# Two layers of a hybrid decoder on one core: norm weights folded into tables, score maps joined, mixer order and both ends rewritten

## The chip, the cores and the metric

The kernel runs on one core of a Trainium2 chip. The metric is the device time of one launch in microseconds (us), as the median of several runs. Where a profile is shown, it is one execution taken by the hardware profiler; its span runs from the first to the last instruction of the program. PE is TensorE, ACT is ScalarE, DVE is VectorE, SP is the queue that issues most transfers.

## What is computed

Two layers, a sequence of 256 positions, a model width of 1024. In each layer the normed input `xn` goes through one joined projection `W_in`, whose columns feed four token mixers; their outputs are gated, summed and projected, and a gated feed-forward block and a gated per-layer embedding follow:

```python
def reference(...):
    for i in range(DEPTH):
        xn = rms_norm(h, norm_mix[i])
        u = xn @ w_in[i]
        (a_x, a_g, b_u, c_q, c_k, c_v, d_q, d_k, d_v, i_q, i_k, i_w) = jnp.split(u, IN_SPLITS, axis=-1)
        o_a = rg_lru_branch(a_x, a_g, ...)            # conv4, gated linear recurrence, GeLU gate
        o_b = conformer_branch(b_u, ...)              # GLU, causal conv31, RMSNorm, swish
        o_c = diff_attention_branch(c_q, c_k, c_v, ...)   # q, k normed with weights, partial rotary
        o_d = sparse_attention_branch(d_q, d_k, d_v, i_q, i_k, i_w, ...)   # indexer, top 64 keys
        mixed = sum(sigmoid(xn @ w_gate[i, j]) * (o_j @ w_branch[i, j]) for j in 0..3)
        h = h + mixed @ w_out[i]
        f = causal_dwconv(rms_norm(h, norm_ffn[i]) @ w_up[i], ...)
        h = h + (silu(f_gate) * f_val) @ w_down[i]
        e = rms_norm(p[i] @ w_ple_in[i], ple_norm[i])
        h = h + sigmoid(rms_norm(h, ple_gate_norm[i]) @ w_ple_gate[i]) * e
    return h
```

## The kernel before

**Products.** Every large product is made of three: both operands are split into a high half `hi` and a rest `lo` of a reduced 32-bit type, and hi·hi, hi·lo and lo·hi are summed. `mm3` (L263, products L271 to L273) holds the weights and streams 256 positions; it serves the units that want channels on the partitions (conformer value and gate `bv`/`bg`, recurrence inputs `a`, the feed-forward `up`). `tok_unit` (L302, products L314 to L316) holds 128 positions and streams 512 weight columns, for both halves `b` of the sequence in turn.

**Weights.** They come as 339 pieces of 128x1024 floats (512 KB). `prep_one` (L203) loads one on SP's queue (L215), makes `hi` by a copy on ACT (L216) and `lo` by a subtraction on DVE (L217). There are five buffers for raw pieces, six for split ones, and `take` keeps three pieces ahead.

**Order.** `unit_list` (L67) sets the order of the units: `bv`/`bg` pairs, the first half of the embedding, `dq`, `dk`, `ik`, `cq`, `ck`, `cv`, eight `a` units, then gates and branches by `MIX_ORDER` (L33), `out`, the second half of the embedding, 22 pairs of `up`, `down`, `pg`. The small work of the mixers (recurrence `side_a` L863, conformer `side_b` L920 with the conv taps L916, differential attention `side_c` L729, sparse attention `side_d` L577) is written as generators. After each piece `pump` (L234) adds 2.6 to each generator's account and lets it take a step for every `EVERY` of its own (L37); before a branch unit `drain` (L247) runs what is left of its mixer. A scheduler then settles the order on each engine from the order of the code and its waits.

**Start.** ACT's queue loads all per-channel vectors of layer 0 (L166, 128x365). On SP's queue come x in four loads of 256 KB (L465), the first piece in two halves, two more pieces, the constants (L469), the four tiles of h (L472), the embedding's gain and its input. Nineteen products of a tile of ones (L188) run ahead. x is multiplied by the norm's weight on ACT (L372, `hi`) and DVE (L373, `lo`); the norm's sums come from squares of h (L360).

**End.** The last unit (`pg`, n=1) sums both halves b over all eight k in turn; then ACT's tanh (L1104), two DVE steps (L1105, L1106) and the output transfers on ACT's queue (L1109) follow, each in two steps of 256 columns:

```python
for c in range(0, 512, step):
    A.activation(t[:, cs], bank[:, cs], AF.Tanh, scale=hr2[:, b:b + 1])
    V.scalar_tensor_tensor(t[:, cs], t[:, cs], 1.0, e[b][n][:, cs], op0=ALU.add, op1=ALU.mult)
    V.scalar_tensor_tensor(h[b][n][:, cs], t[:, cs], re[:, b:b + 1], h[b][n][:, cs], op0=ALU.mult, op1=ALU.add)
    if last:
        nc.scalar.dma_start(out_dram[:, b, n * 512 + c:n * 512 + c + step], h[b][n][:, cs])
```

Of the kernel before, what the change touches and what calls it, by code (L numbers as in the profile page):

```python
# [10 lines left out]
F32 = mybir.dt.float32  # L11
# [21 lines left out]
MIX_ORDER = (("gate", MIX[0]), ("gate", MIX[1]), ("branch", MIX[0]), ("gate", MIX[2]), ("branch", MIX[1]),  # L33
             ("gate", MIX[3]), ("branch", MIX[2]), ("branch", MIX[3]))


EVERY = {0: 4.8, 1: 5.1, 2: 3.3, 3: 2.9, 4: 5.5}  # L37
# [4 lines left out]
for _n, _w in (("norm_mix", 8), ("norm_ffn", 8), ("ple_gate_norm", 8), ("conv_a_w", 16),  # L42
               ("conv_a_b", 4), ("lru_b_r", 4), ("lru_b_i", 4), ("lru_lambda", 4), ("conv_b_w", 124),
               ("conv_b_b", 4), ("conv_b_norm", 4), ("conv_f_w", 132), ("conv_f_b", 44), ("diff_subln", 1)):
    _V[_n] = (_o, _w)
    _o += _w
# [5 lines left out]
for _n, _w in (("diff_q_norm", 64), ("diff_k_norm", 64), ("diff_lq1", 64), ("diff_lk1", 64), ("diff_lq2", 64),  # L52
               ("diff_lk2", 64), ("spa_q_norm", 128), ("spa_k_norm", 128), ("idx_k_norm", 32)):
    _R[_n] = (_o, _w)
    _o += _w
# [11 lines left out]
def unit_list(l):  # L67
# [19 lines left out]
    for n in range(4):  # L87
        bu(n)
    if not l:
        u.append(ple_in[0])  # L90
# [6 lines left out]
    for n in range(8):  # L97
        chan(("a", n), "w_in", n * P)
# [7 lines left out]
    for n in range(2):  # L106
        tok(("out", n), n * 512, n * 512 + 512, "w_out")
    u.append(ple_in[1])
# [15 lines left out]
def decoder_kernel(ctx: ExitStack, tc: tile.TileContext, w_dram, x_dram, xt_dram, p_dram, vec_dram, row_dram,  # L124
# [10 lines left out]
    RAW_BUFS, SPLIT_BUFS, LEAD, NBIG = 5, 6, 3, 37  # L135
# [3 lines left out]
    def nm(s):  # L139
        cnt[0] += 1  # L140
        return f"{s}_{cnt[0]}"

# [11 lines left out]

    def score_banks(Kw):
# [10 lines left out]
    nc.scalar.dma_start(vec[0], vec_dram[0])  # L166
    ones = cst.tile([P, P], F32, name="ones", tag="ones")
    V.memset(ones, 1.0)
    eps = cst.tile([P, 2], F32, name="eps", tag="eps")
# [15 lines left out]

    warm = smbank()
    for _ in range(19):
        T.matmul(warm[:, 0, :], ones, ones, start=True, stop=True)  # L188
# [14 lines left out]
    def prep_one():  # L203
        if nxt[0] >= len(stream):
            return
# [6 lines left out]
        step = m // 2 if i == 0 else m  # L212
        for c in range(0, m, step):
            cs = slice(c, c + step)
            nc.sync.dma_start(raw[:, cs], w_dram[i, :, cs])  # L215
            A.activation(hi[:, cs], raw[:, cs], AF.Copy)  # L216
            last_lo[0] = V.tensor_tensor(lo[:, cs], raw[:, cs], hi[:, cs].bitcast(F32), op=ALU.subtract).ins  # L217
        ready.append((hi[:, :m].rearrange("p (k n) -> p k n", k=nk), lo[:, :m].rearrange("p (k n) -> p k n", k=nk)))

# [121 lines left out]
    def rnorm(acc, scale, bias):  # L341
# [6 lines left out]
        return spread(rt)  # L348

    class Norm:  # L350
# [43 lines left out]

        def half(self):
# [22 lines left out]
    def rope(t, H, W, tab, b):  # L418

        rot = W // 4  # L420
        half = rot // 2
        q = t[:, :, 0:rot]
        cs = tab[:, b, 0, :][:, None, :].to_broadcast([P, H, rot])
        sn = tab[:, b, 1, :]
        t1 = st([P, P], "rp1", 2)[:, :H * rot].rearrange("p (h r) -> p h r", h=H)
        t2 = st([P, P], "rp2", 2)[:, :H * rot].rearrange("p (h r) -> p h r", h=H)
        V.tensor_tensor(t1, q, cs, op=ALU.mult)
        V.tensor_tensor(t2[:, :, 0:half], q[:, :, half:rot], sn[:, None, 0:half].to_broadcast([P, H, half]), op=ALU.mult)
        V.tensor_tensor(t2[:, :, half:rot], q[:, :, 0:half], sn[:, None, half:rot].to_broadcast([P, H, half]), op=ALU.mult)
# [9 lines left out]
    def gain_row(l):  # L439
        t = cst.tile([P, D], F32, name=nm("gain"), tag="gain")  # L440
        nc.sync.dma_start(t, gain_dram[l:l + 1, :].to_broadcast([P, D]))
        return t


    for l in range(L):
        vv = vec[l]
        rr = cst.tile([P, NR], F32, name=nm("row"), tag="row")
        lam_init = 0.8 - 0.6 * math.exp(-0.3 * l)

        def vcol(name):  # L450
            o, w = _V[name]
            return vv[:, o:o + w]
# [5 lines left out]

        if l == 0:
            nxt_nrm = Norm(vcol("norm_mix"))  # L460
            for i in range(4):
                if i == 2:
                    prep_one()
                x_ = bt()
                nc.sync.dma_start(x_, x_dram[:, 2 * i:2 * i + 2, :])  # L465
                nxt_nrm.split(i, x_)
            for _ in range(LEAD - 1):
                prep_one()
            nc.sync.dma_start(con, const_dram)  # L469
            for b in range(2):  # L470
                for n in range(2):
                    nc.sync.dma_start(h[b][n], xt_dram[:, b, n * 512:n * 512 + 512])  # L472
            ph = load_p(0)
        if l == 0:
            gr = gain_row(0)
        pk = [(ph[0][:, k, :], ph[1][:, k, :]) for k in range(2)]
        e = [[None, None], [None, None]]
        se = st([P, 2, 2], "se", 2)

        def embed(n):  # L480
            for b, bank in enumerate(tok_unit(pk, 1)):
                junk = bt().rearrange("p a b -> p (a b)")
                A.activation(junk, bank, AF.Square, accum_out=se[:, n, b:b + 1])
                e[b][n] = bt().rearrange("p a b -> p (a b)")
# [710 lines left out]
```

## Time and profile before

| what | us |
|---|---|
| median of 3 runs | 1048.24 (1047.9 to 1049.01) |
| the profiled execution's own time | 1050.01 |
| its span | 1048.2 |
| PE, DVE, ACT busy in it | 1032.0, 843.3, 690.3 |

The mean granted clock of TensorE in this execution is 0.992 of its full speed. Busy times of PE are modelled from the starts of pipelined products, so a busy PE may still wait inside a product's span; where that matters the starts of two neighbouring products are compared.

### The profile page before, as it was taken

To read this page: it belongs to the slowest core of one execution; us is meant where nothing else is said; L and a number is where in the kernel's file an instruction comes from. 1 tells how busy PE (TensorE), PEld (TensorE's weight loads), DVE (VectorE), ACT (ScalarE), POOL (GpSimd) and SP (SyncE) were. 2 spreads that over 40 slices of the span, in tenths; PEclk is the share of its full clock that TensorE was granted. 3 is DMA by queue.
4 is the path that set the end of the run, shared out by engine and by line. 5 is a ranking of instruction groups with operands and counts; after the bars stand their busy time and mean duration, and the time that the engine had idled before them with its cause. 6 is when DMAs were issued, how large, how long until landed. Compare 5 with 4: busy or idle time off the path is not lost.

```text
span 1048.2 us, 16586 instructions
## 1 busy us (share of the span) xinstructions
PE 1032.0 (98%) x6118; PEld 907.0 (87%) x6118; DVE 843.3 (80%) x1574; ACT 690.3 (66%) x1200; POOL 0.2 (0%) x4
## 2 busy tenths in 40 slices
PE   8999999999999999999999999999999999999997
PEld 7988977788889999988898888777888899999886
DVE  6888999988878978755676889999778799877453
ACT  6765778868557766644675668787784676665443
POOL 0000000000000000000000000000000000000000
PEclk8999999999999999999999999999999999999999
DMA  9765345654765665666656653445556556656641
GB/s 340 270 198 175 113 134 151 191 162 142 219 176 188 182 184 177 187 208 188 187 168 203 188 169 103 137 146 179 161 190 189 164 184 178 187 186 188 189 156 41
DMA packets 52784, 185.42 MB, mean 177 GB/s; under 512 B 5856, under 2 KB 6624, under 8 KB 52704
## 3 DMA queue, kind: packets, MB, share of 16 engines
q1 hardware_dynamic: 51696, 183.14, 56.9%
q10 hardware_dynamic: 1008, 1.24, 0.4%
q8 instruction: 48, 0.79, 0.3%
q14 instruction: 32, 0.26, 0.1%
HBM read 183.30 MB, written 1.05 MB: 176 GB/s over the span
## 4 chain that ended last, share of the span: by engine, by line
PE 82%; DVE 11%; ACT 4%; DMA 1%; issue 1%; SPq 0%; DVEq 0%; ACTq 0%
PE mm L314 17%; PE mm L316 17%; PE mm L315 16%; PE mm L272 9%; PE mm L271 9%; PE mm L273 9%; DVE lo L217 3%; DVE b L916 2%; ACT hi L216 1%; DMA raw<-in_w_dram 1%; DVE s L645 1%; DVE b L854 1%; DVE s L652 1%; PE sp L777 1%; DVE s L651 1%
## 5 line engine op out<-in xcount | busy, mean ns | idle before, releaser
L217 DVE TENSOR_TENSOR lo<-raw,hi 128x1024 fp32r<-128x1024 f32 (+1 forms) x339 | 411.7, 1216 | 142.4 <-ACT hi L216 140.0
L216 ACT ACTIVATE hi<-raw 128x1024 fp32r<-128x1024 f32 (+1 forms) x339 | 355.5, 1055 | 253.0 <-PE mm L316 154.9
L314 PE MATMUL mm<-hi,b 128*128 128x512 f32 x864 | 344.8, 399 | 0.1
L315 PE MATMUL mm<-lo,b 128*128 128x512 f32 x864 | 338.2, 391 | 2.6 <-DVE lo L217 2.6
L316 PE MATMUL mm<-hi,b 128*128 128x512 f32 x864 | 337.6, 391 | 0.0
L271 PE MATMUL mm<-b,hi 128*128 128x256 f32 x976 | 277.6, 286 | 2.3 <-ACT hi L216 1.8
L273 PE MATMUL mm<-b,lo 128*128 128x256 f32 x976 | 276.5, 284 | 1.0 <-DVE lo L217 1.0
L272 PE MATMUL mm<-b,hi 128*128 128x256 f32 x976 | 276.1, 284 | 0.1
L315 PEld LDWEIGHTS mm<-lo,b 128*128 128x128 f32 x864 | 163.0, 189 | 35.8 <-DVE lo L217 3.5
L316 PEld LDWEIGHTS mm<-hi,b 128*128 128x128 f32 x864 | 162.8, 188 | 34.3
L271 PEld LDWEIGHTS mm<-b,hi 128*128 128x128 f32 x976 | 187.5, 193 | 5.4 <-ACT hi L216 2.3
L314 PEld LDWEIGHTS mm<-hi,b 128*128 128x128 f32 x864 | 162.9, 189 | 33.5 <-ACT b L257 1.0
L273 PEld LDWEIGHTS mm<-b,lo 128*128 128x128 f32 x976 | 188.1, 193 | 1.4 <-DVE lo L217 1.4
L272 PEld LDWEIGHTS mm<-b,hi 128*128 128x128 f32 x976 | 187.9, 193 | 0.6 <-DVE b L373 0.4
L916 DVE SCALAR_TENSOR_TENSOR b<-s,vec,b 128x256 f32<-128x256 f32 x240 | 105.0, 477 | 0.0
L1069 DVE SCALAR_TENSOR_TENSOR s<-mm,vec,s 128x255 f32<-128x255 f32 (+1 forms) x144 | 59.5, 474 | 3.0 <-ACT s L1063 3.0
L257 ACT ACTIVATE b<-b 128x512 fp32r<-128x512 f32 x40 | 25.1, 628 | 22.9 <-DVE b L1073 18.5
L258 DVE TENSOR_TENSOR b<-b,b 128x512 fp32r<-128x512 f32 x40 | 27.5, 687 | 11.8 <-ACT b L257 11.8
L1063 ACT ACTIVATE s<-mm,vec 128x256 f32<-128x256 f32 x72 | 36.1, 552 | 0.0
L1072 ACT ACTIVATE s<-s 128x256 f32<-128x256 f32 x44 | 17.8, 409 | 8.7 <-DVE s L1069 8.6
L785 ACT ACTIVATE s<-sp,s,s 128x128 f32<-128x128 f32 (+1 forms) x32 | 16.0, 514 | 8.3 <-DVE s L782 8.3
L989 ACT ACTIVATE b<-mm,s 128x512 f32<-128x512 f32 x32 | 20.9, 690 | 0.8 <-PE mm L316 0.6
(216 smaller groups left out, 763.3 us busy)
## 6 DMA issues: line engine op xcount, KB each, us to landing
raw<-in_w_dram SPq DMA_DIRECT2D x337, 512.0 KB, 4.1
b<-in_x_dram SPq DMA_DIRECT2D x4, 256.0 KB, 6.4
h<-in_xt_dram SPq DMA_DIRECT2D x4, 256.0 KB, 6.2
gain<-in_gain_dram SPq DMA_DIRECT2D x2, 512.0 KB, 5.2
b<-in_lru_dram SPq DMA_DIRECT2D x4, 256.0 KB, 5.1
row<-in_row_dram SPq DMA_DIRECT2D x2, 336.0 KB, 4.5
raw<-in_w_dram SPq DMA_DIRECT2D x2, 256.0 KB, 5.0
b<-in_p_dram SPq DMA_DIRECT2D x2, 256.0 KB, 5.8
```

What stands on the lines that cost most here:

```text
L216: A.activation(hi[:, cs], raw[:, cs], AF.Copy)
L217: last_lo[0] = V.tensor_tensor(lo[:, cs], raw[:, cs], hi[:, cs].bitcast(F32), op=ALU.subtract).ins
L258: V.tensor_tensor(lo, src, hi.bitcast(F32), op=ALU.subtract)
L271: T.matmul(out, a, xh, start=first and k == 0, stop=False)
L272: T.matmul(out, a, xl, start=False, stop=False)
L273: T.matmul(out, b, xh, start=False, stop=last and k == nk - 1)
L314: T.matmul(outs[b], xk[k][0][:, bs], wh[:, kk, :], start=k == 0, stop=False)
L315: T.matmul(outs[b], xk[k][0][:, bs], wl[:, kk, :], start=False, stop=False)
L316: T.matmul(outs[b], xk[k][1][:, bs], wh[:, kk, :], start=False, stop=last)
L916: V.scalar_tensor_tensor(t, ypad[:, c, d:d + S], w[:, 31 * c + d:31 * c + d + 1], t, op0=ALU.mult, op1=ALU.add)
L1063: A.activation(cf[:, 2 * q + s_, :], bank[:, s_, :], AF.Identity, scale=w[:, 3 * c + 2:3 * c + 3], bias=bb[:, c:c + 1])
L1069: V.scalar_tensor_tensor(t, bank[:, s_, :S - d], w[:, 3 * c + 2 - d:3 * c + 3 - d], t, op0=ALU.mult, op1=ALU.add)
```

## The change

1. **Start.** x comes as eight loads of 128 KB, each followed by half a piece of 256 KB; the first four pieces hold two rows of k for four channel groups each (`bvg`), so that four `bv`/`bg` units run together, k by k. Only the norm's weight (128x8) is loaded ahead on ACT's queue; vectors, most constants, h, embedding input and gain come later. Ten products of ones instead of nineteen. The first norm's sums are taken from x in channel layout (`channel_finish`: squares, sums and a product with ones). The first half of the embedding of layer 0 moves behind the `out` units.
2. **Norm weights.** The q and k weights of both attentions are folded into the rotation tables and, for the columns that are not rotated, into the scale of the copy after the transpose. The multiplications L668 and L751 go; `rope` makes one product on a swapped view instead of two. The softmax scale goes into the per-head scale.
3. **Score maps.** For the first half of the sequence the indexer's two groups and the four heads of the differential attention each share banks and instructions.
4. **Order.** The `a` units move ahead of `dq`; `side_a` starts there. Gates 0, 3 and 2 come ahead of the first branch. `EVERY[2]` is 3.4 and `EVERY[3]` 3.2 (3.3 and 2.9 before). Layer 1's small values are made at the end of layer 0. Big buffers: 43 instead of 37.
5. **End.** The last unit makes half b=0 whole, then b=1 in two parts of 256 columns, each over all k (`tok_parts`); the outputs are issued by SP.

```diff
-MIX_ORDER = (gate 0, gate 3, branch 0, gate 2, branch 3, gate 1, branch 2, branch 1)
+MIX_ORDER = (gate 0, gate 3, gate 2, branch 0, gate 1, branch 3, branch 2, branch 1)
@@ unit_list
+        u.append((("bvg", 0), "w_in", [(k, 2, [(c, c + P) for c in (1024, 1536, 1152, 1664)]) for k in range(0, KD, 2)]))
+    for n in range(8):
+        chan(("a", n), "w_in", n * P)
     tok(("tok", "dq"), 3584, 4096)
...
-    for n in range(8):
-        chan(("a", n), "w_in", n * P)
@@ start
-    for _ in range(19):
+    for _ in range(10):
         T.matmul(warm[:, 0, :], ones, ones, start=True, stop=True)
...
+            nxt_nrm = Norm(gain0)
+            for k in range(KD):
+                if k % 2 == 0:
+                    x0.append(bt())
+                dma(x0[-1][:, k % 2, :], x_dram[:, k, :])
+                nxt_nrm.split(k // 2, x0[-1], (k % 2,))
+                prep_part()
...
+                for q in range(4):
+                    mm3(bbanks[q // 2][:, q % 2, :], wk, xs, q * P, k == 0 and q % 2 == 0, k + 1 == KD and q % 2 == 1)
...
+                if (l, c, j) == (0, 2, 0):
+                    nrm.channel_finish(x0)
@@ rope
-        V.tensor_tensor(t2[:, :, 0:half], q[:, :, half:rot], ...)
-        V.tensor_tensor(t2[:, :, half:rot], q[:, :, 0:half], ...)
+        V.tensor_tensor(t2.rearrange(two, u=2), q.rearrange(two, u=2)[:, :, ::-1, :], sn.rearrange(two, u=2), op=ALU.mult)
@@ side_d heads, side_c heads
-                for hh in range(4):
-                    q = dq[b][:, hh * P:(hh + 1) * P]
-                    V.scalar_tensor_tensor(q, q, ms[:, b, hh:hh + 1], rcol("spa_q_norm"), op0=ALU.mult, op1=ALU.mult)
...
-                V.tensor_tensor(v3, v3, rcol(gain)[:, None, :].to_broadcast([P, 8, 64]), op=ALU.mult)
...
+                    A.activation(dst[m][:, :, b * P:(b + 1) * P], tp[:, 2 * m:2 * m + 2, :], AF.Copy,
+                                 scale=vcol(f"diff_{gain}_col"))
@@ side_c
-            for b in range(2):
-                yield from weave(attend(b, hp) for hp in range(2))
+            yield from weave([*two_heads(1), attend(0, (0, 1))])
+            yield from weave(attend(1, (hp,)) for hp in range(2))
@@ end
+    def tok_parts(xk, npieces):
+        pcs = take(npieces)
+        for b, c, n in ((0, 0, 512), (1, 0, 256), (1, 256, 256)):
...
+            yield b, c, bank
...
-                        nc.scalar.dma_start(out_dram[:, b, n * 512 + c:n * 512 + c + step], h[b][n][:, cs])
+                        for dst, src in outs:
+                            nc.sync.dma_start(dst, src)
```

How the instructions stand at three places, before and after. First SP's queue at the start of the program: `raw` is a piece of weights, `b` from `in_x_dram` is x, `con` the constants, `h` the residual. Before:

```order
L465 DMA b_106<-in_x_dram 128x512
L215 DMA raw_122<-in_w_dram 128x512 x2
L215 DMA raw_147<-in_w_dram 128x1024
L215 DMA raw_153<-in_w_dram 128x1024
L465 DMA b_114<-in_x_dram 128x512
L469 DMA con<-in_const_dram 128x610
L472 DMA h_70<-in_xt_dram 128x512
L472 DMA h_71<-in_xt_dram 128x512
L472 DMA h_72<-in_xt_dram 128x512
L465 DMA b_131<-in_x_dram 128x512
```

After, from the last pair of x and weights on (seven such pairs, 128x256 and 128x512, stand ahead of it):

```order
L150 DMA b_152<-in_x_dram 128x256
L150 DMA raw_158<-in_w_dram 128x512
L150 DMA con<-in_const_dram 128x128
L150 DMA raw_200<-in_w_dram 128x1024
L150 DMA vec_75<-in_vec_dram 128x368
L150 DMA raw_231<-in_w_dram 128x1024
L150 DMA raw_261<-in_w_dram 128x1024
L150 DMA raw_292<-in_w_dram 128x1024
L150 DMA con<-in_const_dram 128x482
```

The wide loads of constants, vectors and h between the pieces have moved behind the last of x; h stands further down than these rows.

Second DVE in layer 0, in the stretch where the two attentions and the recurrence run beside the token units, at the rotation of one key or query tile. Before (L651 and L652 are the top-k search, L883 and L885 the recurrence, L217 the next piece's `lo`):

```order
L651 MAX s_1622<-s_1212 128x8
L751 TENSOR_TENSOR b_857<-b_857,row_104 128x512
L652 MATCH_REPLACE s_1213<-s_1622,s_1212 128x256
L427 TENSOR_TENSOR s_1629<-b_857,con 128x128
L651 MAX s_1625<-s_1213 128x8
L428 TENSOR_TENSOR s_1630<-b_857,con 128x8x8
L652 MATCH_REPLACE s_1212<-s_1625,s_1213 128x256
L429 TENSOR_TENSOR s_1630<-b_857,con 128x8x8
L883 SCALAR_TENSOR_TENSOR b_1550<-b_1550,b_1172 128x512
L430 TENSOR_TENSOR b_857<-s_1629,s_1630 128x8x16
L885 SCALAR_TENSOR_TENSOR b_1552<-b_1551,b_1552 128x512
L217 TENSOR_TENSOR lo_1649<-raw_1647,hi_1648 128x1024
```

After, at the same kind of tile (L491 to L493 are the rotation, L1002 the conformer's taps, L747 the top-k search, L538 a small value, L233 `lo`):

```order
L1002 SCALAR_TENSOR_TENSOR b_509<-s_172,vec_75,b_509 128x256 x2
L1002 SCALAR_TENSOR_TENSOR b_510<-s_172,vec_75,b_510 128x256 x2
L747 MATCH_REPLACE s_1480<-s_1656,s_1481 128x128
L491 TENSOR_TENSOR s_1671<-b_1297,s_503 128x128
L492 TENSOR_TENSOR s_1672<-b_1297,s_503 128x128
L233 TENSOR_TENSOR lo_1684<-raw_1682,hi_1683 128x1024
L493 TENSOR_TENSOR b_1297<-s_1671,s_1672 128x8x16
L491 TENSOR_TENSOR s_1727<-b_1184,s_501 128x128
L492 TENSOR_TENSOR s_1728<-b_1184,s_501 128x128
L538 TENSOR_TENSOR s_4938<-s_4938 128x4
L493 TENSOR_TENSOR b_1184<-s_1727,s_1728 128x8x16
L233 TENSOR_TENSOR lo_1709<-raw_1707,hi_1708 128x1024
```

The weight product ahead of the rotation is gone, the rotation is three rows instead of four, and the recurrence's rows are not there any more: they stand among earlier units. Two `lo` stand among these twelve rows, where one stood.

Third ACT in layer 0 at the conformer's norm, which needs the squares of two tiles (L928 before, L1014 after) and whose sums PE then makes. Before (L836 copies attention outputs, L989 is a gate's tanh):

```order
L836 ACTIVATE b_2613<-sp_2645,s_442 128x2x128
L836 ACTIVATE b_2615<-sp_2645,s_442 128x2x128
L216 ACTIVATE hi_2749<-raw_2748 128x1024
L836 ACTIVATE b_2613<-sp_2680,s_442 128x2x128
L836 ACTIVATE b_2615<-sp_2680,s_442 128x2x128
L216 ACTIVATE hi_2773<-raw_2772 128x1024
L928 ACTIVATE b_2731<-b_534 128x512
L928 ACTIVATE b_2732<-b_535 128x512
L216 ACTIVATE hi_2799<-raw_2798 128x1024
L989 ACT_TABLE_LOAD
```

After (L914 is a root, L921 the scaling of the differential attention's heads, L291 a split):

```order
L914 ACT_TABLE_LOAD
L914 ACTIVATE s_1858<-s_1858,eps 128x8
L1014 ACTIVATE b_2647<-b_509 128x512
L921 ACTIVATE b_1856<-b_1856,s_1858 128x128 x4
L291 ACTIVATE b_2266<-sp_2604 128x2x128
L921 ACTIVATE b_1857<-b_1857,s_1858 128x128 x3
L291 ACTIVATE b_2268<-sp_2604 128x2x128
L921 ACTIVATE b_1857<-b_1857,s_1858 128x128
L1014 ACTIVATE b_2648<-b_510 128x512
L232 ACTIVATE hi_2698<-raw_2697 128x1024
L232 ACTIVATE hi_2733<-raw_2732 128x1024
L389 ACTIVATE s_2656<-sp_2653,eps 128x2
```

The two squares stood next to each other; now the second stands behind eight scalings and two splits.

## Rows read from the trace of the kernel before

**Rows 1.** The page, part 1: engine, busy us (share of the span) xinstructions.
```profile
PE 1032.0 (98%) x6118; PEld 907.0 (87%) x6118; DVE 843.3 (80%) x1574; ACT 690.3 (66%) x1200; POOL 0.2 (0%) x4
```

**Rows 2.** Windows by stage: stretch, us, busy of each engine, PEclk, DMA share, GB/s.
```profile
0.00:20.00 20.00, 15.97 (x90) 14.71 (x91) 12.51 (x46) 10.88 (x20) 0.20 (x4) 0.83 0.92 339
100.00:140.00 40.00, 40.00 (x279) 36.16 (x278) 39.70 (x101) 31.10 (x59) 0.00 (x0) 1.00 0.38 118
140.00:230.00 90.00, 87.20 (x429) 69.45 (x428) 85.19 (x202) 68.11 (x151) 0.00 (x0) 0.98 0.54 162
656.00:746.00 90.00, 87.30 (x429) 69.59 (x428) 84.25 (x195) 67.97 (x151) 0.00 (x0) 0.98 0.53 158
```

**Rows 3.** Windows of the main products alone (tile mm), columns as in 2.
```profile
0.00:20.00 20.00, 9.98 (x52) 8.91 (x53) 0.00 (x0) 0.00 (x0) 0.83 0.92 339
340.00:440.00 100.00, 100.00 (x836) 100.00 (x835) 28.84 (x69) 17.04 (x34) 1.00 0.63 184
450.00:470.00 20.00, 20.00 (x90) 16.54 (x89) 0.00 (x0) 0.00 (x0) 1.00 0.70 213
```

**Rows 4.** Timeline of the start: start us, us, engine line operation [idle before <-releaser].
```profile
1.04 5.99 PE L188 MATMUL sp<-ones 128*128 128x128 f32 x38 [1.04 <-DVE ones L168]
7.15 0.39 PE L271 MATMUL mm<-b,hi 128*128 128x256 f32 x1
...
10.44 0.39 PE L271 MATMUL mm<-b,hi 128*128 128x256 f32 x1 [1.82 <-ACT hi L216]
...
12.03 0.58 PE L273 MATMUL mm<-b,lo 128*128 128x256 f32 x1 [0.75 <-DVE lo L217]
```

**Rows 5.** Windows of 2 us in the start, columns as in 2.
```profile
10.00:12.00 2.00, 0.85 (x3) 0.48 (x3) 1.93 (x6) 1.58 (x5) 0.00 (x0) 0.76 1.06 389
12.00:14.00 2.00, 1.97 (x9) 1.97 (x10) 1.79 (x9) 0.45 (x2) 0.00 (x0) 0.50 1.06 404
16.00:18.00 2.00, 1.92 (x10) 1.90 (x10) 1.49 (x6) 1.46 (x3) 0.00 (x0) 0.54 1.02 400
```

**Rows 6.** Waits of PE: waited for, us in total, times, longest us.
```profile
PE sp L777 <- ACT s L785: 2.9, 2, 1.5
PE mm L315 <- DVE lo L217: 2.6, 2, 1.3
```

**Rows 7.** Timeline at the wait on an exp, columns as in 4.
```profile
170.13 0.71 PE L777 MATMUL sp<-b,b 64*128 64x128 f32 x4 [1.49 <-ACT s L785]
```

**Rows 8.** Lines by form, DVE: line engine op names shapes xcount | busy us, mean ns | idle.
```profile
L751 DVE TENSOR_TENSOR b<-b,row 128x512 f32<-128x512 f32 x8 | 5.4, 679 | 0.0
L668 DVE SCALAR_TENSOR_TENSOR b<-b,s,row 128x128 f32<-128x128 f32 x16 | 4.8, 342 | 0.0
L428 DVE TENSOR_TENSOR s<-b,con 128x64 f32<-128x64 f32 x12 | 2.6, 213 | 0.0
L854 DVE SCALAR_TENSOR_TENSOR b<-b,vec,b 128x255 f32<-128x255 f32 x8 | 3.8, 477 | 0.0
```

**Rows 9.** Lines by form, ACT: columns as in 8.
```profile
L827 ACT ACTIVATE b<-b,s 128x128 f32<-128x128 f32 x16 | 4.9, 389 | 2.0 <-DVE s L821 2.0
L820 ACT ACT_TABLE_LOAD x2 | 2.6, 1283 | 0.0
L928 ACT ACTIVATE b<-b 128x512 f32<-128x512 f32 x4 | 2.3, 624 | 1.6 <-DVE b L916 1.6
```

**Rows 10.** Timeline of the end, columns as in 4.
```profile
1041.70 1.57 ACT L1104 ACTIVATE b<-mm,s 128x256 f32<-128x256 f32 x4 [9.51 <-PE mm L316]
...
1041.95 0.39 PE L316 MATMUL mm<-hi,b 128*128 128x512 f32 x1
...
1043.42 2.28 ACTq L1109 DMA_DIRECT2D out_dram<-h  x4
...
1044.38 0.87 DVE L1106 SCALAR_TENSOR_TENSOR h<-b,s,h 128x256 f32<-128x256 f32 x2
```

More of the change, by code (lines that the diff above doesn't have):

```diff
@@ L86, in unit_list @@
         u.append(ple_in[0])
[L87 to L90, printed above, removed]
+    if l:
+        bu(0)
+        bu(1)
+    else:
+        u.append((("bvg", 0), "w_in", [(k, 2, [(c, c + P) for c in (1024, 1536, 1152, 1664)]) for k in range(0, KD, 2)]))
+    bu(2)
+    bu(3)
+    for n in range(8):
+        chan(("a", n), "w_in", n * P)
     tok(("tok", "dq"), 3584, 4096)
@@ L323, in tok_unit @@
         return outs
+    def tok_parts(xk, npieces):
+        pcs = take(npieces)
+        for b, c, n in ((0, 0, 512), (1, 0, 256), (1, 256, 256)):
+            bank = mmbank().rearrange("p a b -> p (a b)")[:, :n]
+            bs, cs = slice(b * P, (b + 1) * P), slice(c, c + n)
+            k = 0
+            for wh, wl in pcs:
+                for kk in range(wh.shape[1]):
+                    last = k + 1 == len(xk)
+                    for q, (x_, w_) in enumerate(((0, wh), (0, wl), (1, wh))):
+                        tc.keep_in_program_order(T.matmul(bank, xk[k][x_][:, bs], w_[:, kk, cs],
+                                                          start=k == 0 and q == 0, stop=last and q == 2))
+                    k += 1
+            yield b, c, bank
     def fold(acc):
@@ L393, in finish, with channel_finish @@
             root(self.rt, self.ss[:, 0, :], 1.0 / D, eps[:, 0:1])
+        def channel_finish(self, xs):
+            sq = []
+            for x in xs:
+                sq.append(bt())
+                A.activation(sq[-1], x, AF.Square)
+                if len(sq) > 1:
+                    V.tensor_tensor(sq[0], sq[0], sq[-1], op=ALU.add)
+            fold(sq[0])
+            self.rt, self.rs2 = rnorm(sq[0], 1.0 / D, eps[:, 0:1])
+            self.rs2 = self.rs2[:, None, :].to_broadcast([P, 2, S])
         def half(self):
@@ L943, in side_b @@
                 yield
-        for c in range(4):
-            evac_b(nrm.scaled(bbanks[c]), c)
-        if not l:
-            embed(0)
         conv_y = [bt() for _ in range(2)]
@@ L952, in decoder_kernel @@
         side(1, side_b(), EVERY[1])
+        lw = [bt().rearrange("p a (b c) -> p (a b) c", b=2) for _ in range(2)]
+        for i in range(2):
+            dma(lw[i], lru_dram[l, :, 4 * i:4 * i + 4])
+        for fn in (evac_a, evac_ga):
+            for i in range(2):
+                bank = mmbank()
+                for j in range(2):
+                    chan_unit(bank, j, xsk, 1)
+                    pump()
+                fn(nrm.scaled(bank), i)
+        side(0, side_a(), EVERY[0])
         evac_tok("dq")
```

414 lines of the change are left out of this document (230 added, 184 removed).

## The prediction

> **What bounds the kernel now.** The page's busy line comes first: PE is busy for 1032.0 of 1048.2 us, DVE for 80% of the span, ACT for 66% [rows 1]. The number of large products does not change, so the change can win only what PE spends waiting, on a low clock, or ahead of and behind the products. The windows by stage say where that is [rows 2]. Three places stand out. In 0 to 20 us PE has 15.97 us of work, much of it products of ones and at a clock of 0.83. In 140 to 230 and again in 656 to 746, one layer later, PE has gaps (2.80 and 2.70 us), the clock reads 0.98, and DVE has 85.19 and 84.25 us of work in 90; in the 40 us ahead it has 39.70. The third place is the end [rows 10]. Elsewhere PE runs through: a 256-column product starts every 100 / 836 = 0.120 us, a 512-column one every 20 / 90 = 0.222 us [rows 3].
>
> **The start.** By 20 us only 52 large products have started [rows 3], worth 52 x 0.120 = 6.2 us; so 13.8 us of the first 20 are lost. The timeline shows how [rows 4]: the products of ones end at 7.03 and the first large one starts at 7.15, then PE waits 1.82 us for a `hi` and 0.75 for a `lo`. Behind these waits the clock falls: 0.76 in 10 to 12, 0.50 in 12 to 14, back in 16 to 18 [rows 5], 6.8 us at half in all. The transfers are at their limit all the while, 389 to 404 GB/s [rows 5], so bytes and their order decide.
>
> The change puts less ahead of the first product. Before, it needed the vectors (187 KB), 256 KB of x and 256 KB of weights; now 4 KB, 128 KB and 256 KB. That is 0.32 MB less, 0.8 us at 0.4 MB per us, and one half of the weight multiplication of x on ACT, some 0.2 us, goes with it: first product at about 6.15. After it a pair of x and weights (0.39 MB) lands every 1.0 us, and each pair feeds 12 products, 12 x 0.120 = 1.44 us. ACT and DVE each have two instructions on a pair, by the conformer square in [rows 9] at most 0.62 us each, which fits 1.44. So PE should run through from 6.15, and the lost time becomes 6.15 and some 0.25 for the first `lo`: 6.4 instead of 13.8, **-7.4 us**. The loads that are moved behind (constants, vectors, later h and the gain) are queued on SP behind the last of x; the next pieces are wanted only every 24 x 0.120 = 2.9 us there and take 1.3 us each, so they cover about as much again. The first norm's sums now come from ACT and DVE work in the same stretch; the first recurrence unit waits for a bank that they free, but that unit comes 8 x 1.44 = 11.5 us and four further units (11.5 us) later; I cost that at nothing, and at up to 0.5 us if the cover is gone. Ends: -7.9, if the first x lands earlier still, and -4.4, if the clock falls once (below).
>
> **The middle.** The time lost is read from windows: 2.80 us of gaps in layer 0 and 2.70 in layer 1, and half clock for 0.02 x 90 / 0.5 = 3.6 us in each, which loses 1.8 us at most. That is 4.5 per layer, **9.0 us** in both. Two waits explain the gaps [rows 6]: a `lo` (2.6 us, two of them, 1.3 each) and an exp (2.9, two, up to 1.5); the timeline shows the second at 170.13 [rows 7], and the clock falls behind it.
>
> The waits on `lo` come from DVE's load. Per layer the change takes away eight 128-column weight products, 8 x 0.342 = 2.7, four of 512, 4 x 0.679 = 2.7, and one 0.213 step in each of some twelve rotations less what the wider one takes, say 1.3 [rows 8]: 6.7 us. It moves the recurrence's taps, 12 x 0.477 = 5.7 us [rows 8], with its other steps, from the crowded stretch to earlier units, where the windows show room only behind 20 us; that is the second order excerpt. Together some 12 us leave a stretch in which DVE lacked perhaps 2. I take the waits on `lo` as gone, and the exp wait too: it stood where three mixers ran together, and one of them is now over earlier.
>
> What is late next? The third excerpt shows it: the second square of the conformer's norm stands on ACT behind a table load, a root, eight scalings and two splits. From the attention product that releases this run to that square, ACT has 1.28 + 8 x 0.389 + 2 x 0.624 [rows 9] and seven smaller ones of about 0.39, 8.4 us by their mean durations; DVE's sum and fold add about 1.1. ACT instructions overlap: at the end of the trace four of a kind take 1.57 us [rows 10], 0.39 each, where one lasts 0.475 (that factor, 0.83, on 9.5 gives 7.9). PE has 28 products of 0.222 and two small ones ahead of its sums there, 6.7 us. So a new wait of 1.2 us per layer; from 0, if the run starts earlier, to 2.8 by full durations, and 4.5 if the `hi` copy and split ahead of it count as well. I take 1.2, since back-to-back rows of this trace overlap, and 0.3 for banks that the recurrence now wants earlier: 3.0 in both layers. Net **-6.0 us** (ends -9.0 and 0).
>
> **The end.** The last product starts at 1041.95, and DVE's last step ends at 1045.25 [rows 10], 3.30 later: two banks of 512 columns end together, and four pieces go through ACT, DVE and DVE in turn. Now only 256 columns are left behind the last product: one tanh (0.475), two DVE steps of about 0.4 and 0.45, and a start of 0.3, 1.6 us. That saves 1.7, less the price of halving: 48 x 0.120 - 24 x 0.222 = 0.4. **-1.3 us** (ends -0.5, if the five transfers on SP line up at 2.28 / 4 = 0.57 each behind the last step, and -1.7).
>
> **The sum.** -7.4 - 6.0 - 1.3 = -14.7 on a span of 1048.2 gives 1033.5. The profiled execution's own time is 1050.01, 1.8 above its span and 1.77 above the median of the runs; the same step puts the changed one at 1035.3 in a profile and at 1048.24 - 14.7 = **1033.5** in the median.
>
> **Rivals.**
>
> *The clock falls in the start.* Ten products of ones are 20 of the 38 passes in [rows 4]: by an even share of their 5.99 us they end at 4.2, and later if the first ones are the slow ones. I take 4.8, so PE waits for 1.35 us until 6.15. Before, the clock fell behind a wait of 1.82 us [rows 4, 5] and, in the middle, behind one of 1.49 [rows 7]; 0.98 over 90 us [rows 2] leaves room for no second fall there, so none came behind the `lo` wait of 1.3 [rows 6]. A fall of the length of the start's, 6.8 us, costs about 3.0: 1036.5. The Trainium skill, "TensorE: Matmul & The Clock Gate", section "HAM oscillation — how this bites in real kernels", says the same against the change: a wait for a transfer between products drops TensorE to its low clock, and the work behind it starts cold. By that rule the fewer products of ones would be a loss; this trace agrees at 10 to 12 us, where the clock fell to 0.76 behind such a wait. Chance 0.15.
>
> *The middle's waits come back elsewhere.* DVE's busy time falls only by some 13 of 843 us, and the moved recurrence meets the conformer's taps in 100 to 140, where DVE has 39.70 of 40. If each wait removed returns once, only the start and the end are won: 1048.24 - 7.4 - 1.3 = 1039.5. Against it: the sum of the stretch from 140 on does fall. Chance 0.16.
>
> *Slower: ACT becomes the bound of the mixers.* Place: the run of roots, scalings and exps around the three gates. Price per layer: 4.5 for the square, 1.0 for banks, 0.4 for exps, and behind each of three such waits a half clock that loses up to 1.8 as now, 11.3 us; both layers 22.6 against 8.7 + 9.0 = 17.7 won: 1048.24 + 4.9 = 1053.1. It decides from 8.9 us of new waits per layer. Against it: ACT has only 68.11 of 90 us of work there [rows 2]. Chance 0.05.
>
> *The change cancels.* The start's second pair is as late as now (SP issues twice as many loads), 4 us are lost to new waits per layer, and little is left: within 0.2% of 1048.24. Chance 0.04.
>
> **How the numbers follow.** The forecast, 1028 to 1038 with its bounds, has 0.60. A range of 1028 to 1041 takes in nearly all of it, of the first rival, and of the second up to 1.5 us beyond its value; left out are the sum of both, the last two, and gains above 20 us. A change of less than 0.2% (2.1 us) can't be told from none here. Faster: 0.60 + 0.15 + 0.16, 0.91; same 0.04; slower 0.05.
>
> **What would show it.** Right: the first large product near 6.15 and about 110 by 20 us; the waits of PE list no `lo` of DVE above 0.5 us in the middle; a wait of about 1.2 us at the product with ones of the conformer's norm, behind ACT's square; DVE's last step 1.6 us behind the last product. Wrong: PEclk of 0.5 in a window before 20 us (first rival), a `lo` or exp wait of over 1 us between 100 and 250 us (second), or ACT as the releaser of more than 9 us of PE's waits per layer (third).

## The result, and the profile after

The changed kernel takes 1031.96 us (median of 4 runs, 1031.66 to 1032.21) against 1048.07 for the kernel before (4 runs): ratio 0.9846, 95% interval 0.9833 to 0.9858, so 16.1 us faster; 1033.5 was forecast. The profiled execution has a span of 1029.9 us; its busy line and the windows by stage (columns as in rows 2):

```profile
PE 1023.2 (99%) x6124; PEld 901.0 (87%) x6124; DVE 832.9 (81%) x1526; ACT 691.0 (67%) x1190; POOL 0.2 (0%) x4
```
```profile
0.00:20.00 20.00, 18.48 (x131) 18.07 (x132) 13.53 (x37) 15.62 (x29) 0.20 (x4) 1.00 0.85 298
100.00:140.00 40.00, 40.00 (x196) 31.79 (x195) 39.68 (x102) 29.03 (x52) 0.00 (x0) 1.00 0.70 224
140.00:230.00 90.00, 90.00 (x460) 73.72 (x459) 81.90 (x205) 67.57 (x151) 0.00 (x0) 1.00 0.51 159
656.00:746.00 90.00, 90.00 (x456) 73.01 (x455) 78.24 (x190) 68.68 (x156) 0.00 (x0) 1.00 0.51 158
```

Against [rows 2], PE is busy in all of 140 to 230 and of 656 to 746 at full clock, where 2.8 and 2.7 us were missing at 0.98; DVE has 81.90 of 90 us there instead of 85.19, and still 39.68 of 40 ahead of it. The list of PE's waits (columns as in rows 6; `mm` are the tiles of the large products, `sp` those of the small ones) has nothing over 0.3 us behind the first product of ones; the waits at L315 and L777 [rows 6] are gone:

```profile
PE sp L383 <- DVE s L390: 0.3, 1, 0.3
PE mm L305 <- ACT hi L232: 0.3, 1, 0.3
PE mm L307 <- DVE lo L233: 0.2, 1, 0.2
PE mm L305 <- DVE b L428: 0.2, 1, 0.2
```

In the start 107 large products have begun by 20 us where 52 had [rows 3]; the timeline shows what paces them (PE, and ACT's work on x, L424, and on weights, L232):

```profile
0.00:20.00 20.00, 13.98 (x107) 13.43 (x108) 0.00 (x0) 0.00 (x0) 1.00 0.85 298
```
```profile
5.33 0.56 PE L305 MATMUL mm<-b,hi 128*128 128x256 f32 x1
...
5.74 0.63 ACT L232 ACTIVATE hi<-raw 128x512 fp32r<-128x512 f32 x1 [0.67 <-DMA raw<-in_w_dram]
...
7.63 0.51 ACT L424 ACTIVATE b<-b,gain 128x256 fp32r<-128x256 f32 x1 [1.25 <-DMA b<-in_x_dram]
...
8.31 0.63 ACT L232 ACTIVATE hi<-raw 128x512 fp32r<-128x512 f32 x1 [0.17 <-DMA raw<-in_w_dram]
...
8.99 0.39 PE L305 MATMUL mm<-b,hi 128*128 128x256 f32 x1 [0.25 <-ACT hi L232]
...
9.36 0.63 ACT L232 ACTIVATE hi<-raw 128x512 fp32r<-128x512 f32 x1
...
9.72 0.38 PE L307 MATMUL mm<-b,lo 128*128 128x256 f32 x1 [0.23 <-DVE lo L233]
```

The first product is at 5.33. The third half piece is split at 8.31, 2.57 us behind the second, since its pair lands late; from there on they come every 1.0 us (9.36, 10.39, 11.38). PE waits for 0.25 and 0.23 us, and the clock does not fall. At the end one part of 256 columns is left behind the last product:

```profile
1022.05 5.33 SPq L1210 DMA_DIRECT2D out_dram<-h  x3
...
1025.25 0.28 PE L371 MATMUL mm<-hi,b 128*128 128x256 f32 x1
1025.57 0.47 ACT L1203 ACTIVATE b<-mm,s 128x256 f32<-128x256 f32 x1 [2.40 <-PE mm L371]
...
1026.54 0.49 DVE L1205 SCALAR_TENSOR_TENSOR h<-b,s,h 128x256 f32<-128x256 f32 x1
```

DVE's last step ends at 1027.03, 1.78 behind the start of the last product (3.30 before, [rows 10]).

The table takes each profile apart. The loss by 20 us is 20 less the worth of the large products begun by then (0.120 and 0.227 us each, the spacing of neighbouring starts; the count behind the 0.222 of [rows 3] takes in a product that reaches over the window's end); the loss between is the start of the last product less the worth of all of them (940 us) and less the loss by 20; it holds the small products too, in all kernels. Medians are of 4 to 10 runs; the first two kernels were timed together, and over all 47 runs beside the other kernels the one before has a median of 1049.33. The losses are of one execution each: of one above the median in the kernel before (1050.01), of the fastest or nearly so in the three kernels made from it (1047.64, 1044.90 and 1050.56). The runs of one kernel spread by 0.2 to 1.5 us where the clock does not fall, so medians less than some 0.5 us apart are not told from equal; and the seven executions with the start of the changed kernel as it is lose between 7.0 and 7.8 by 20 us.

| kernel | median us | loss by 20 | loss between | behind the last product's start |
|---|---|---|---|---|
| before | 1048.07 | 13.8 | 88.4 | 6.27 |
| changed | 1031.96 | 7.2 | 78.0 | 4.62 |
| weights back | 1032.39 | 7.2 | 78.9 | 4.61 |
| old gates | 1037.42 | 7.0 | 83.9 | 4.62 |
| recurrence late | 1043.09 | 7.3 | 88.5 | 4.83 |
| recurrence late, weights back | 1043.93 | 7.5 | 89.7 | 4.83 |
| all three | 1043.40 | 7.0 | 89.6 | 4.85 |
| old end | 1033.23 | 7.8 | 77.9 | 6.21 |
| vectors first | 1032.68 | 8.1 | 77.9 | 4.70 |
| 1 product of ones | 1032.06 | 7.0 | 78.0 | 4.62 |
| 19 products of ones | 1032.35 | 7.4 | 79.0 | 4.62 |
| before, recurrence early | 1049.13 | 12.9 | 86.9 | 6.28 |
| before, no weights | 1046.69 | 12.8 | 84.3 | 6.28 |
| before, both orders | 1052.26 | 12.9 | 89.6 | 6.28 |

### The profile page after: what moved, and what is told of

It is laid out like the page before. It is cut to its first block, busy times and chain, and to the rows that moved or that the text cites. A ratio compares the mean times of both kernels' runs of the same rounds, so it can differ in the third digit from the quotient of the medians.

```text
span 1029.9 us, 16561 instructions
## 1 busy us (share of the span) xinstructions
PE 1023.2 (99%) x6124; PEld 901.0 (87%) x6124; DVE 832.9 (81%) x1526; ACT 691.0 (67%) x1190; POOL 0.2 (0%) x4
## 4 chain that ended last, share of the span: by engine, by line
PE 96%; ACT 2%; DVE 1%; DMA 1%; SPq 0%; issue 0%; ACTq 0%
PE mm L348 18%; PE mm L349 18%; PE mm L350 18%; PE mm L307 11%; PE mm L305 11%; PE mm L306 11%; PE mm L371 1%; PE sp L439 1%; PE sp L873 1%; PE sp L729 1%; PE sp L789 1%; PE sp L903 1%; DMA raw<-in_w_dram 1%; ACT b L921 0%; ACT hi L232 0%; PE sp L847 0%
## 5 line engine op out<-in xcount | busy, mean ns | idle before, releaser
L232 ACT ACTIVATE hi<-raw 128x1024 fp32r<-128x1024 f32 (+1 forms) x342 | 354.9, 1048 | 210.8 <-PE mm L350 126.6
L233 DVE TENSOR_TENSOR lo<-raw,hi 128x1024 fp32r<-128x1024 f32 (+1 forms) x342 | 410.0, 1207 | 102.1 <-ACT hi L232 99.7
L348 PE MATMUL mm<-hi,b 128*128 128x512 f32 x848 | 337.5, 399 | 0.1
L349 PE MATMUL mm<-lo,b 128*128 128x512 f32 x848 | 331.1, 391 | 0.0
L350 PE MATMUL mm<-hi,b 128*128 128x512 f32 x848 | 330.2, 390 | 0.0
L307 PE MATMUL mm<-b,lo 128*128 128x256 f32 x976 | 275.7, 283 | 0.2 <-DVE lo L233 0.2
L348 PEld LDWEIGHTS mm<-hi,b 128*128 128x128 f32 x848 | 159.2, 188 | 35.8 <-issue 1.8
L350 PEld LDWEIGHTS mm<-hi,b 128*128 128x128 f32 x848 | 159.2, 188 | 33.7
L307 PEld LDWEIGHTS mm<-b,lo 128*128 128x128 f32 x976 | 186.9, 192 | 0.6 <-DVE lo L233 0.6
L349 PEld LDWEIGHTS mm<-lo,b 128*128 128x128 f32 x848 | 159.5, 188 | 31.5 <-issue 0.5
L1002 DVE SCALAR_TENSOR_TENSOR b<-s,vec,b 128x256 f32<-128x256 f32 x240 | 105.4, 477 | 0.0
L291 ACT ACTIVATE b<-b 128x512 fp32r<-128x512 f32 x40 | 25.0, 626 | 21.8 <-DVE b L1168 19.1
L292 DVE TENSOR_TENSOR b<-b,b 128x512 fp32r<-128x512 f32 x40 | 27.4, 687 | 12.6 <-ACT b L291 12.6
L479 DVE TENSOR_TENSOR b<-mm,s 128x512 f32<-128x512 f32 x24 | 16.3, 684 | 11.1 <-PE mm L307 11.0
```

What stands on the lines that cost most here:

```text
L292: V.tensor_tensor(lo, src, hi.bitcast(F32), op=ALU.subtract)
L307: T.matmul(out, b, xh, start=False, stop=last and k == nk - 1)
L348: T.matmul(outs[b], xk[k][0][:, bs], wh[:, kk, :], start=k == 0, stop=False)
L349: T.matmul(outs[b], xk[k][0][:, bs], wl[:, kk, :], start=False, stop=False)
L350: T.matmul(outs[b], xk[k][1][:, bs], wh[:, kk, :], start=False, stop=last)
L1002: V.scalar_tensor_tensor(t, ypad[:, c, d:d + S], w[:, 31 * c + d:31 * c + d + 1], t, op0=ALU.mult, op1=ALU.add)
```

## The experiments

**Which part of the change carries the middle?** Four kernels undo parts of it in the changed kernel. The first moves the recurrence back:

```diff
-    for n in range(8):
-        chan(("a", n), "w_in", n * P)
     tok(("tok", "dq"), 3584, 4096)
...
     tok(("tok", "cv"), 3072, 3584)
+    for n in range(8):
+        chan(("a", n), "w_in", n * P)
```

(and the code that runs these units and starts `side_a` goes behind `side(2, side_c(), ...)`.)

> The changed kernel with the eight recurrence units back behind cv. Theory (the crowded DVE stretch costs the waits, and the moved recurrence is the larger part of the relief): DVE is again over 84 of 90 us busy somewhere between 140 and 230 us, at least one wait on a lo half or an exp of over 1 us per layer returns, +2 to +6 us on 1032.0. Rival (the three gates ahead of the first branch are what gave room): within 1 us of 1032.0, no such wait.

Measured: 1043.09, +11.1 us, more than either side expected; DVE is at 82.17 of 90 us, not over 84, and no wait on a `lo` half or an exp returns. PE's waits show one new entry, and the windows a fall of the clock; the last rows are from the timeline at the wait:

```profile
PE sp L895 <- DVE s L889: 8.4, 2, 4.2
```
```profile
140.00:230.00 90.00, 85.77 (x430) 69.10 (x429) 82.17 (x200) 70.72 (x163) 0.00 (x0) 0.98 0.49 153
```
```profile
159.47 0.39 PE L349 MATMUL mm<-lo,b 128*128 128x512 f32 x1
...
163.69 1.12 DVE L889 SCALAR_TENSOR_TENSOR s<-s,s 128x128 f32<-128x128 f32 x4
...
164.08 0.74 PE L895 MATMUL sp<-con,s 128*128 128x128 f32 x2 [4.23 <-DVE s L889]
...
164.47 0.77 PE L350 MATMUL mm<-hi,b 128*128 128x512 f32 x1
```

L895 are the transposes of the differential attention's probabilities; they wait 4.2 us in each layer for DVE's weighted difference L889, whose turn comes late, and the next large product starts only behind them (164.47, the one ahead at 159.47). So here it is not a `lo` half that is late, but a small step of a mixer.

The second puts the weights back as products with ones:

```diff
+                for hh in range(4):
+                    q = dq[b][:, hh * P:(hh + 1) * P]
+                    V.scalar_tensor_tensor(q, q, ones[:, hh:hh + 1], ones, op0=ALU.mult, op1=ALU.mult)
...
+                V.tensor_tensor(v3, v3, ones[:, None, 0:64].to_broadcast([P, 8, 64]), op=ALU.mult)
                 rope(v3, 8, 64, tabs[f"diff_{gain}"][:, b])
```

(`rope` has its two half products again.)

> The changed kernel with the multiplications by q and k weights and the two-part rotation put back as products with ones (same shapes and counts as before, some 6.7 us of DVE work per layer). Theory: a smaller part of the relief, +0 to +3 us on 1032.0, a wait on a lo half of up to 1 us per layer. Rival (gates): within 1 us. If the weights were the whole relief: +6 to +9.

Measured: 1032.39, +0.4 us, at the low end and within the spread of the runs (1032.16 to 1032.62 beside 1031.66 to 1032.21). DVE has 84.78 us of work in 140 to 230 there, nearly the 85.19 of [rows 2], and PE has no wait over 0.3 behind the first product of ones:

```profile
140.00:230.00 90.00, 89.85 (x456) 73.31 (x455) 84.78 (x227) 66.52 (x149) 0.00 (x0) 1.00 0.52 158
```

A DVE as full as before does not by itself cost time here. The third has both edits.

> Both of the former: recurrence units behind cv and the multiplications back, with the new order of gates kept. Theory: most of the middle's gain goes, +6 to +10 us on 1032.0, with waits on lo halves and exps of over 1 us and a clock fall in 140 to 230 us. Rival (gates): under +2 us.

Measured: 1043.93, +12.0 us, more than expected, and 0.8 on top of the late recurrence: the move decides, the weights add little. The wait on the weighted difference is 3.1 us per layer, and a `lo` half is waited for again (2.1 us, two of them, 1.0 each); the clock reads 0.96 in 140 to 230. The fourth has `MIX_ORDER` and `EVERY` of before.

> The changed kernel with the order of gates and branches and the two EVERY values of before. Theory (DVE load): the relief stays, +0 to +2 us on 1032.0, from waits on exps as the mixers have to end earlier. Rival (gates): +5 to +9 us, the waits at L873 behind the exp and on lo halves return.

Measured: 1037.42, +5.5 us, at the rival's end, without a fall of the clock. The waits are at other places than expected: three in the last steps of the sparse attention ahead of its branch (L808 copies its transposed probabilities, L813 makes its output, L291 and L292 split it for the branch), and in layer 0 one of the differential attention's transposes (L895) behind a copy of the sparse attention's queries (L770):

```profile
PE mm L350 <- DVE b L292: 1.6, 2, 0.8
PE sp L813 <- ACT b L808: 1.3, 2, 0.7
PE sp L895 <- ACT b L770: 1.1, 1, 1.1
...
PE mm L348 <- ACT b L291: 0.8, 2, 0.4
```

**All three undone.** The edits of the three before, together.

> The changed kernel with all three undone: recurrence units behind cv, multiplications by weights and two-part rotation back, order of gates and EVERY of before. Left of the change are the start, the joined maps and the end. Theory: start and end are worth 8.7 us, so 1048.2 - 8.7 = 1039.5, that is +7 to +9 on 1032.0, with the waits of the kernel before (a lo half and an exp of 1.3 to 1.5 us, a clock fall in each layer). Rival (the new order of gates is good only with the early recurrence, and the old one was tuned to the late one): the same 1039.5, below the 1043.9 of late recurrence with the new gates. If the joined maps carry part of the middle's gain: 1036 to 1038.

Measured: 1043.40, +11.4 us. Both sides had 1039.5, 3.9 too low; the rival holds only in so far as late recurrence with old gates is not worse than with the new ones. In its profile the start and the end lose nearly what they lose in the changed kernel (7.0 and 4.85 in the table), but the loss between is 89.6, no less than the 88.4 of the kernel before; so with the orders of before no gain of the joined maps shows. The orders form a square: with the weights back, late with old gates 1043.4 and late with new 1043.9; without them, early with old 1037.4 and early with new 1032.0. The new gates are worth nothing while the recurrence is late (0.5 the other way, within the spread), and 5.5 us once it is early. Two of the waits are again on small steps (transposes L773 behind a part of the rotation, L494, and L853 behind a gate of the recurrence, L976), the third on a `lo` half:

```profile
PE sp L773 <- DVE s L494: 3.8, 2, 2.2
PE sp L853 <- ACT b L976: 2.4, 2, 1.5
PE mm L349 <- DVE lo L233: 1.8, 2, 0.9
```

**Parts alone, on the kernel before.** First the move of the recurrence:

```diff
+    for n in range(8):
+        chan(("a", n), "w_in", n * P)
     tok(("tok", "dq"), 3584, 4096)
```

> The kernel before with one part of the change alone: the eight recurrence units and the start of the recurrence moved ahead of dq; gates as before. Theory (the move is what relieves the crowded stretch): the waits on lo halves and on L785's exp are gone, -4 to -9 us against the kernel before. Rival (the parts work only together, as undoing the gates alone cost 5.4): -0 to -4 us, with the waits on copies ahead of the drained branches that the run with the old gates showed.

Measured: 1049.13 beside 1048.58, ratio 1.0013 (1.0000 to 1.0027): no gain, so the theory fell. The waits on `lo` and exp in the mixers are gone, but the loss between falls only from 88.4 to 86.9 (in a fast execution), and a wait stands where the differential attention ends (L833, behind the scalings L827):

```profile
PE sp L833 <- ACT b L827: 1.6, 2, 0.8
...
PE mm L314 <- ACT b L257: 0.6, 2, 0.4
```

Second the weights left out (L668 and L751 removed, one of them with the per-head scale in it):

> The kernel before with the multiplications by the q weights of the sparse attention and the q and k weights of the differential attention left out (L668, L751), nothing else; so the per-head scale and the weights are missing from the result. Theory of the prediction (5.4 us of DVE work per layer out of a stretch that is full): both waits on lo halves go or halve, -2 to -5 us. Rival (the weights are worth as little as in the changed kernel, 0.4): within 1 us.

Measured: 1046.69, ratio 0.9977 (0.9966 to 0.9987), -1.9 us: between the two. The waits on `lo` halves at L315 have gone; the scores of the differential attention (L773) wait behind a `lo` instead, 1.7 us per layer:

```profile
PE sp L773 <- DVE lo L217: 3.3, 2, 1.7
...
PE sp L773 <- ACT s L781: 0.8, 2, 0.4
```

Third both orders together, with the 43 buffers (and the smaller transfer scratch that makes room for them):

```diff
+MIX_ORDER = (gate 0, gate 3, gate 2, branch 0, gate 1, branch 3, branch 2, branch 1)
+EVERY = {0: 4.8, 1: 5.1, 2: 3.4, 3: 3.2, 4: 5.5}
+    for n in range(8):
+        chan(("a", n), "w_in", n * P)
     tok(("tok", "dq"), 3584, 4096)
```

> The kernel before with both orders of the change alone: the recurrence units and the start of the recurrence ahead of dq, three gates ahead of the first branch with the new EVERY values, and the 43 big buffers that the gates' tiles take. Start, weights, maps and end as before. Theory (the two orders carry the middle, and only together: on the new start they took 1043.4 to 1032.4): 11 us off, 1048.6 - 11.0 = 1037.6, no wait of over 1 us in the mixers. Rival (weights and maps are needed with them): 1042 to 1046, with waits on DVE left between 100 and 250 us.

Measured: 1052.26 beside 1049.33, ratio 1.0026 (1.0017 to 1.0036): slower by 2.9 us. Both theories fell. The mixers' stretch is free of waits (PE 90.00 of 90 us in 140 to 230), and new ones stand behind it:

```profile
PE sp L345 <- DVE b L326: 3.1, 2, 1.6
...
PE sp L833 <- ACT b L827: 1.7, 2, 0.8
```
```profile
140.00:230.00 90.00, 90.00 (x455) 72.59 (x454) 84.49 (x224) 62.84 (x143) 0.00 (x0) 1.00 0.51 157
230.00:300.00 70.00, 67.48 (x306) 53.49 (x305) 52.03 (x81) 45.70 (x81) 0.00 (x0) 0.98 0.51 158
```
```profile
L833 PE MATMUL sp<-con,b x16: 328/330/475, 261.3 to 779.6; 128*128 128x128 f32 x16
```

L345 makes the sums of the conformer's norm, the product at which the prediction set a wait of 1.2 for the changed kernel; here it is 1.6 us per layer, but not behind the run that the prediction names: the scalings of the differential attention come only ahead of L833. That is the attention's end; it runs from 261.3 on (from 241.7 in the kernel before), and the clock falls behind it (0.98). Where it stands follows from the code. `side_c` has 32 steps before, and takes one for every 3.4 / 2.6 pieces: 41.8 pieces. From its start to the branch that drains it there were 48 pieces while the recurrence units came behind cv; with them moved ahead 40 are left, so its end is drained at once. The move alone leaves 40 pieces for 32 x 3.3 / 2.6 = 40.6, and there L833 starts at 261.2. In the changed kernel the four heads that share instructions leave 28 steps, 36.6 pieces, and its end stands well ahead of the drain:

```profile
L927 PE MATMUL sp<-con,b x16: 270/272/273, 238.9 to 755.3; 128*128 128x128 f32 x16
```

So the joined maps are the likely reason that the two orders pay in the changed kernel. That step is counted from the code and read from these rows; no run undid the joined maps alone, so it is not shown, and the waits at L833 itself are only 0.8 us per layer. Not tested either: the other parts that differ between these two kernels (the start, small values of layer 1 made at the end of layer 0).

**The start.** Three kernels. All vectors loaded first again:

```diff
-    nc.scalar.dma_start(gain0, vec_dram[0][:, o_:o_ + KD])
+    nc.scalar.dma_start(vec[0], vec_dram[0])
```

> The changed kernel with all vectors of layer 0 (188 KB) loaded first on ACT's queue again instead of the 4 KB of norm weights, and not later. Theory (bytes ahead of the first product decide): the first product 0.4 to 0.9 us later than 5.33, +0.4 to +1.0 us on 1032.0, more if the gap behind the products of ones lowers the clock (+1 to +3). Rival (fixed cost of the first transfers decides): the first product within 0.2 us of 5.33, no change of the time.

Measured: 1032.68, +0.7 us; first product at 5.75, 0.42 later. The theory holds for the size, but not quite for the place. Two waits are listed; the one at L307 is not of the vectors, since the run with the old end has it too (0.5, with the start unchanged), the other is new and stands at the first norm's sums (L396; the chain that was costed at 0 to 0.5):

```profile
PE mm L307 <- DVE lo L233: 0.5, 1, 0.5
PE sp L396 <- DVE b L377: 0.4, 1, 0.4
```

> The changed kernel with one product of ones instead of ten. Theory: PE is idle until 5.33, starts at the low clock, and the clock rises some us later: +1.5 to +3 us on 1032.0, a window at 0.50 between 5 and 10 us. Rival (what PE does ahead of the first product does not matter): within 0.3 us.

```diff
-    for _ in range(10):
+    for _ in range(1):
```

Measured: 1032.06, +0.1 us: the rival. PE did start at the low clock, as expected, with 11 products in 6 to 8 us (19 in the changed kernel, last row). PEclk reads 1.00 there all the same, since the trace has the granted clock only from its first rise on (9.04 here); what shows it is the spacing of the products, 0.21 us until 8.9 and 0.12 from 9.2 on. The first product was at 4.68, and no later one waited in the start:

```profile
6.00:8.00 2.00, 2.00 (x11) 2.00 (x11) 0.00 (x0) 0.00 (x0) 1.00 0.89 262
0.00:20.00 20.00, 15.12 (x108) 14.94 (x109) 0.00 (x0) 0.00 (x0) 1.00 0.87 302
```
```profile
6.00:8.00 2.00, 2.00 (x19) 2.00 (x19) 0.00 (x0) 0.00 (x0) 1.00 0.93 306
```

> The changed kernel with nineteen products of ones, as before. Theory: nine more at 0.112 to 0.213 us for each of two passes keep PE until 6.5 to 7.0, so the first product is 1.2 to 1.7 us later, but pairs are then ahead and two waits of 0.25 us go: +0.7 to +1.5 us on 1032.0. Rival (more products of ones bring the clock up earlier and pay for themselves): -0.5 to +0.2 us.

Measured: 1032.35, +0.4 us, between the two and within the spread; the first product is at 7.23, 1.9 us later, and 105 products have begun by 20 us all the same:

```profile
0.00:20.00 20.00, 12.77 (x105) 12.72 (x106) 0.00 (x0) 0.00 (x0) 1.00 0.87 292
```

First products at 4.68, 5.33 and 7.23 give losses of 7.0, 7.2 and 7.4, no further apart than executions of one start. So in this range neither the first product decides nor the clock ahead of it: what PE gains by an earlier one it gives back, to the low clock with one product of ones and to two waits for the third pair in the changed kernel; with nineteen it has no wait left there.

**The end.** The last unit and the outputs of before.

> The changed kernel with the last unit and the outputs of before (both halves of 512 columns in turn, four steps of 256 columns behind them, outputs on ACT's queue). Theory: +1.3 us on 1032.0, the last DVE step 3.3 us behind the last product. Rival (the end was given back by the transfers that line up on SP): within 0.5 us.

Measured: 1033.23, +1.3 us, as expected; 6.21 us behind the last product's start instead of 4.62, for 0.3 less in products.

## Why the prediction was right

**The sum** came out 1.5 us short (1033.5 for 1031.96), inside the range. The start and the end were sized right within 0.8 us. The middle was not: -6.0 was forecast, and the loss between fell by 10.4 in the profiles. That the median came so near is partly luck: the profiled execution of before, whose rows the losses are taken from, was 1.9 us above its median.

**The start, -7.4.** The profiles give 13.8 to 7.2, -6.6; the three kernels that keep the start of before lose 12.8 to 12.9, where the clock fell for half as long (PEclk 0.91 in 0 to 20 instead of 0.83). The step "so PE should run through from 6.15, and the lost time becomes 6.15 and some 0.25" had the parts wrong: the first pair is ready at 4.7 and the first product at 5.33, but 1.9 us are lost behind it, mostly to the low clock until 5.99 and around the two waits. The term "a pair lands every 1.0 us" holds only from the third pair, which came 2.57 us behind the second. Removing bytes was right (188 KB more cost 0.7 us), and so was "costed at nothing, up to 0.5 us" for the first norm. The first rival, the fall of the clock, did not come: the first pair was ready 1.5 us earlier than the 6.15 that it rests on, and in none of the seven executions with this start did PE wait between the products of ones and the first large one. By the Trainium skill, "TensorE: Matmul & The Clock Gate", section "HAM oscillation — how this bites in real kernels", work behind a wait for a transfer starts cold. The run with one product of ones agrees in so far as the products behind its wait of 2.8 us ran at the low clock (11 in 2 us instead of 19); but there the clock had not risen before, and no price of it shows in the time (1032.06 for 1031.96).

**The middle, -9.0 + 3.0.** Both waits and both falls of the clock went, as the term of 9.0 said. The term that failed is the +3.0 for "What is late next?". The run on ACT is there, in the predicted order and length: from the copy behind the attention product to the end of DVE's fold it takes 8.1 us for the 7.9 of the sum. What was too small is PE's own work ahead of the sums, "28 products of 0.222 and two small ones", 6.7 us: four products of the sparse attention (L813) stand among them, PE reaches its sums (L396) 8.2 us behind that copy, and the list of waits has no entry there:

```profile
227.86 0.39 ACT L905 ACTIVATE b<-sp 128x256 f32<-128x256 f32 x1 [0.42 <-PE sp L903]
...
230.42 1.88 PE L813 MATMUL sp<-b,b 128*128 128x512 f32 x4
...
234.15 0.62 ACT L1014 ACTIVATE b<-b 128x512 f32<-128x512 f32 x1
...
235.53 0.43 DVE L377 TENSOR_TENSOR b<-b 128x256 f32<-128x256 f32 x1
...
236.10 0.58 PE L396 MATMUL sp<-ones,b 128*128 128x1 f32 x4
```

It is close: the sums start 0.14 us behind the fold's end, and 0.52 behind the last large product where 0.227 is usual, so some 0.3 per layer may still be lost. With that in place of the 3.0, -9.0 + 0.6, the forecast would have been 1031.1.

The cause was wrong too. "Together some 12 us leave a stretch in which DVE lacked perhaps 2" made it a matter of DVE's load, with the weights for more than half. DVE's work fell by 3.3 us only in 140 to 230 and by 6.0 in 656 to 746. The weights are worth 0.4 there, within the spread (1.9 alone, on the kernel before); the same load put back cost nothing while the order was kept. What the runs point to is when the mixers' small steps come due on PE against the piece count: the order of gates, which the sum priced at nothing, is worth 5.5, the move of the recurrence 11.1, and both together on the kernel before cost 2.9. The second rival (waits come back elsewhere) is what that last run shows, at the conformer's norm and at the end of the differential attention; that it did not decide here because the attention has fewer steps is counted, not shown.

**The end, -1.3.** Measured +1.3 when undone; 1.78 us behind the last product for the 1.6 that were worked out, and the five transfers did not line up.

**The sum of the parts.** In the profiles the stages give 6.6 + 10.4 + 1.65 less 0.3 for the 24 more products, 18.3, as the spans do (1048.2 to 1029.9). The medians moved by 16.1, since the profiled execution of before was a long one, above its own median by 1.9 (last section).

## What to carry to other kernels

A wait is often set by the schedule that releases a small step, not by the load of its engine; so count the releases: steps of a generator times their price against the pieces until its drain. Moving units ahead of it takes pieces away from it, and fewer steps can give them back. Edits of an order that gain nothing alone can gain together, so each is tried with the edit that may make room for it. When a following step is costed, count all of PE's work ahead of it, the small products too: here four of them hid most of a predicted wait. In this start neither the first product nor the clock ahead of it was worth tuning; the bytes ahead of the pairs were.

## What the runs showed that was not expected

The kernel before spreads over 5.0 us (1046.37 to 1051.32 in 47 runs), the changed one over 0.6 in four, and the time goes with the granted clock: of the 47 runs, 10 had a mean clock of 0.992 and a median of 1050.14 us, 22 had 0.995 and 1049.23, 9 had 0.997 and 1046.54 (the other six read 0.994 or 0.996). The changed kernel had 0.999 to 1.000 in all runs and 1031.66 to 1032.21. So the clock falls more in some runs of one and the same program than in others; which waits it fell behind is seen in the profiled execution alone. By that the waits that were removed would be worth more in some runs than in others.

The clock's first rise is not at a fixed place either. The trace has it at 4.2 us in the profile of before, at 5.99 in the changed kernel, at 9.04 with one product of ones, and between 3.93 and 7.11 in the seven executions with one and the same start. Those two lost 7.0 and 7.2 us by 20, so no price of it shows in the start.
